# A decoder trunk's attention: where the first query tile's scores and values stand in TensorE's order

## Chip, cores and metric

One Trainium2 chip, one of its cores. The metric is the device time of one execution in microseconds (us), as the median of several runs. Beside it there is one execution taken by the hardware profiler; all rows of engines, waits and instructions come from that one. In the profile PE is TensorE (PEld its weight loads), DVE is VectorE, ACT is ScalarE, POOL is GpSimd and SP is SyncE. "L730" is line 730 of the kernel.

## The reference

Two layers over a sequence of 512 rows of width 1024, in float32. Each layer is a mixer and then a gated MLP with a short convolution, each between two RMS norms. The mixer projects its input once, and the columns feed three groups: four heads of differential attention, four of retention, and a pooling mixer. Only the attention is touched here:

```python
def block(args):
    q_blk, i = args                      # one tile of 128 queries
    s = jnp.einsum('bhmqd,bhmkd->bhmqk', q_blk, k) * scale   # m: two maps per head
    p = jax.nn.softmax(jnp.where(mask, s, -jnp.inf), axis=-1)
    a = p[:, :, 0] - lam * p[:, :, 1]
    return jnp.einsum('bhqk,bhkd->bhqd', a, v)
...
o = rms_norm(o, subln_g) * (1.0 - lam_init)
```

A head has two score maps; the second softmax is taken from the first, times a learned factor, and the difference weighs the values. The mask is causal, so query tile 0 sees only key tile 0, tile 1 two of them, and so on.

## The kernel before

All large products are done as three TensorE products of split operands (high x high, high x low, low x high), 128 x 128 by 512 columns each; these are the main products. A layer has 2256 of them: 480 for the input projection, 192 for the output projection, 1056 up and 528 down. The input projection goes through five blocks of 96: queries (products 0 to 96), keys (96 to 192), values (192 to 288), retention's queries to values (288 to 384), gates and pooling (384 to 480).

Attention and retention are small work, put between the main products. TensorE's order is fixed: every product and every turn (a transpose on TensorE) gets a dependency on the one before (`in_order`, L332). The small work comes as generators, the tasks. Each yields a place, counted in main products, and the names of what must be done ahead of it. After each group of three main products `serve` runs those that are due, the one with the earliest place first:

```python
def serve(columns=0):
    now[0] += columns / 512
    while True:
        due = [tk for tk in tasks if tk[1] <= now[0] and all(n in done for n in tk[2])]
        if not due:
            return
        with ahead(300):
            resume(min(due, key=lambda tk: tk[1]))
```

The places are read from the table `PLACE` (L45), the same for both layers, offset by 2256. So a place that has passed, or lies ahead of the time when its task is created, means "at the next group". The other engines' order is made by the scheduler of the framework from priorities and a model of times; only TensorE's is written out.

The tasks of attention, for a query tile i and a head h (in the order of tiles, then heads):

- "a", `scores` and `unit_a` (L716): two short TensorE products for one map (high and low part of the queries), in one of two PSUM banks in turn; then DVE adds the mask (L730) and takes the row maximum (L731), ACT the exponential with its sums (L733). After the second map DVE joins the two (L738 to L740).
- "b", `turns` and `unit_b` (L742): TensorE turns the joined weights, ACT copies them to SBUF (L749). It waits in order for the values two heads before.
- "c", `values` and `unit_c` (L752): TensorE multiplies the turned weights with the values. All four heads of a tile share one bank, kept for this. After head 3 the tile is normalised: four squares with sums on ACT (L766), then a row of small DVE operations (L767, and L394 to L402 in `rsqrt`), and L770 writes the normalised tile.
- "e", `outputs` and `unit_e` (L781): TensorE turns that normalised tile, and it is split into the output projection's operand.

The tasks are created after the key block, at product 192. The queries and keys of each tile are turned and split by tasks of their own ("Q", "K" in the first layer, "q", "k" in the second; `qk_done` L636, `q_split` L658, `k_split` L667); a score needs those of the tiles it sees, and at least tiles 0 and 1. Weights come over SP's queue as tiles of 512 KB, three in flight, and are split by ACT (L300) and DVE (L301) as the main products free their slots.

Of the kernel before, what the change touches and what calls it, by code (L numbers as in the profile page):

```python
# [54 lines left out]
    ],  # L55
    "b": [[234, 235, 232, 242], [275, 278, 280, 287], [326, 334, 338, 320], [381, 385, 388, 418]],
    "c": [[241, 236, 242, 243], [282, 260, 284, 296], [330, 342, 326, 350], [386, 402, 397, 427]],
    "e": [264, 317, 373, 452],
    "rows": 404,
    "r1": [395, 431, 465, 513],  # L60
# [1137 lines left out]
```

## Time and profile before

| | |
|---|---|
| median of 3 runs | 1148.23 us (1146.52 to 1148.41) |
| the profiled execution, time | 1146.27 us |
| its span, first to last instruction | 1144.5 us |
| TensorE busy | 1133.6 us, 99% of the span |
| DVE busy | 738.4 us, 65% |
| ACT busy | 547.9 us, 48% |
| DMA, mean over the span | 95 GB/s |
| mean granted TensorE clock | 0.999 |

The span runs from the first to the last instruction; the time has what lies around it too. In timeline rows the first number is the start in us from the span's start, the second the length in us; "out<-in" are the kernel's names of tiles, "x3" merges three instructions in a row, and the brackets tell how long the engine stood idle before the row and what it waited for. Matmuls are pipelined, and their ends are modelled, so the distance from start to start is the measure of what a product costs on TensorE.

### The profile page before, as it was taken

To read this page: it belongs to the slowest core of one execution; us is meant where nothing else is said; L and a number is where in the kernel's file an instruction comes from. 1 tells how busy PE (TensorE), PEld (TensorE's weight loads), DVE (VectorE), ACT (ScalarE), POOL (GpSimd) and SP (SyncE) were. 2 spreads that over 40 slices of the span, in tenths; PEclk is the share of its full clock that TensorE was granted. 3 is DMA by queue.
4 is the path that set the end of the run, shared out by engine and by line. 5 is a ranking of instruction groups with operands and counts; after the bars stand their busy time and mean duration, and the time that the engine had idled before them with its cause. 6 is when DMAs were issued, how large, how long until landed. Compare 5 with 4: busy or idle time off the path is not lost.

```text
span 1144.5 us, 14829 instructions
## 1 busy us (share of the span) xinstructions
PE 1133.6 (99%) x5474; PEld 944.9 (83%) x5474; DVE 738.4 (65%) x1667; ACT 547.9 (48%) x1051; POOL 11.9 (1%) x20
## 2 busy tenths in 40 slices
PE   9999999999999999999999999999999999999997
PEld 7788878988888888888888888789888888888886
DVE  6988796776566457423777896876856655663224
ACT  6965544564454345313367754454645434452221
POOL 1000000000000000000000000000000000000000
PEclk9999999999999999999999999999999999999999
DMA  8411131332322333324023111313333233223311
GB/s 327 146 58 56 56 116 38 111 129 97 107 92 92 99 104 97 96 93 146 1 98 123 56 57 54 111 39 117 121 99 104 81 104 103 100 76 109 96 50 58
DMA packets 31320, 109.22 MB, mean 95 GB/s; under 512 B 3728, under 2 KB 4240, under 8 KB 31248
## 3 DMA queue, kind: packets, MB, share of 16 engines
q1 hardware_dynamic: 29808, 105.11, 27.5%
q10 hardware_dynamic: 1440, 3.17, 0.8%
q8 instruction: 43, 0.70, 0.3%
q14 instruction: 29, 0.24, 0.1%
HBM read 106.16 MB, written 2.10 MB: 95 GB/s over the span
## 4 chain that ended last, share of the span: by engine, by line
PE 94%; DVE 3%; ACT 2%; issue 0%; DMA 0%; DVEq 0%; ACTq 0%
PE ps L338 74%; PE ps_m L338 12%; PE ps_o L338 2%; PE ps_b L338 2%; PE ps_b L341 2%; PE ps_s L338 1%; PE ps L341 1%; DVE ks L670 1%; ACT t L733 0%; DMA raw<-in_wout 0%; DVE sm L731 0%; DVE ps_s L730 0%; ACT ks L669 0%; ACT t L642 0%; ACT wa L300 0%
## 5 line engine op out<-in xcount | busy, mean ns | idle before, releaser
L338 PE MATMUL ps<-ht,wb 128*128 128x512 f32 (+1 forms) x1176 | 304.8, 368 | 0.0
L338 PE MATMUL ps<-ht,wa 128*128 128x512 f32 (+1 forms) x1176 | 304.7, 367 | 0.0
L338 PEld LDWEIGHTS ps<-ht,wa 128*128 128x128 f32 x1176 | 210.3, 188 | 36.5
L338 PEld LDWEIGHTS ps<-ht,wb 128*128 128x128 f32 x1176 | 210.2, 189 | 36.6
L301 DVE SCALAR_TENSOR_TENSOR wa<-raw,par,wa 128x512 fp32r<-128x512 f32 x128 | 95.7, 748 | 142.6 <-ACT wa L300 142.3
L300 ACT ACTIVATE wa<-raw,par 128x512 fp32r<-128x512 f32 x128 | 92.1, 721 | 185.0 <-PE ps L338 173.4
L338 PE MATMUL ps<-wa,c 128*128 128x512 f32 x448 | 126.2, 393 | 0.0
L290 DVE TENSOR_TENSOR wb<-raw,wa 128x1024 fp32r<-128x1024 f32 x38 | 46.5, 1225 | 81.9 <-ACT wa L289 81.9
L338 PEld LDWEIGHTS ps<-wa,c 128*128 128x128 f32 x448 | 83.6, 188 | 18.0 <-issue 1.0
L301 DVE SCALAR_TENSOR_TENSOR wb<-raw,par,wb 128x512 fp32r<-128x512 f32 x128 | 95.6, 747 | 4.0 <-ACT wb L300 3.8
L338 PE MATMUL ps<-wa,ht 128*128 128x512 f32 x352 | 97.9, 392 | 0.0
L300 ACT ACTIVATE wb<-raw,par 128x512 fp32r<-128x512 f32 x128 | 91.9, 719 | 4.3 <-PE ps L338 3.1
L338 PE MATMUL ps_m<-wa,ht 128*128 128x512 f32 x288 | 83.6, 398 | 1.8 <-ACT t L642 1.8
L338 PE MATMUL ps_m<-wb,ht 128*128 128x512 f32 x288 | 83.3, 397 | 0.0
L289 ACT CAST wa<-raw 128x1024 fp32r<-128x1024 f32 x38 | 39.9, 1051 | 86.7 <-PE ps L338 86.7
L1068 ACT ACTIVATE t<-ps,par 128x512 f32<-128x512 f32 x88 | 67.4, 773 | 24.9 <-PE ps L338 24.9
L338 PEld LDWEIGHTS ps<-wa,ht 128*128 128x128 f32 x352 | 66.2, 189 | 13.9 <-issue 0.4
L1069 DVE SCALAR_TENSOR_TENSOR t<-ps,par,t 128x511 f32<-128x511 f32 x88 | 65.2, 745 | 11.8 <-ACT t L1068 11.7
L338 PE MATMUL ps<-wb,c 128*128 128x512 f32 x224 | 71.8, 397 | 0.0
L338 PE MATMUL ps<-wb,ht 128*128 128x512 f32 x224 | 66.2, 389 | 0.0
L1070 DVE SCALAR_TENSOR_TENSOR t<-ps,par,t 128x510 f32<-128x510 f32 x88 | 65.0, 745 | 1.3
L338 PEld LDWEIGHTS ps_m<-wb,ht 128*128 128x128 f32 x288 | 52.5, 188 | 10.1
(194 smaller groups left out, 1415.3 us busy)
## 6 DMA issues: line engine op xcount, KB each, us to landing
raw<-in_wup SPq DMA_DIRECT2D x88, 512.0 KB, 3.5
raw<-in_wdown SPq DMA_DIRECT2D x44, 512.0 KB, 3.4
raw<-in_win SPq DMA_DIRECT2D x39, 512.0 KB, 3.6
raw<-in_wout SPq DMA_DIRECT2D x16, 512.0 KB, 3.4
xs<-in_x SPq DMA_DIRECT2D x4, 512.0 KB, 9.1
gain<-in_gpost ACTq DMA_DIRECT2D x4, 512.0 KB, 4.1
t<-in_xt SPq DMA_DIRECT2D x3, 512.0 KB, 5.7
out<-xs SPq DMA_DIRECT2D x4, 256.0 KB, 2.0
```

The source lines that it names most:

```text
L289: se.copy(h, r)
L290: ve.tensor_tensor(out=lo, in0=r, in1=h.bitcast(F32), op=ALU.subtract)
L300: se.activation(a, x, AF.Copy, scale=sc)
L301: low = ve.scalar_tensor_tensor(b, x, sc, a.bitcast(F32), op0=ALU.mult, op1=ALU.subtract)
L338: in_order(te.matmul(out, lhsT=lhsT, rhs=rhs, **k))
L341: in_order(te.transpose(out, in_, ident))
L670: ve.tensor_tensor(out=ks[o, :, m, sl], in0=bv[r], in1=ks[r, :, m, sl].bitcast(F32), op=ALU.subtract)
L1068: se.activation(acc, ps, AF.Identity, bias=conv[:, f, 3:4], scale=conv[:, f, 2:3])
L1069: ve.scalar_tensor_tensor(acc[:, 1:S], ps[:, 0:S - 1], conv[:, f, 1:2], acc[:, 1:S], op0=ALU.mult, op1=ALU.add)
L1070: ve.scalar_tensor_tensor(acc[:, 2:S], ps[:, 0:S - 2], conv[:, f, 0:1], acc[:, 2:S], op0=ALU.mult, op1=ALU.add)
```

## The change

Six numbers of the table move, nothing else. For query tile 0 the first score (head 0, first map) goes from place 152 to 199. Turns of heads 2 and 3 go from 232 and 242 to 242 and 246. Values of heads 1, 2 and 3 go from 236, 242 and 243 to 244, 249 and 253. Head 0's turn and value (234, 241), head 1's turn (235), all other scores and the other query tiles stay, and so does the turn of tile 0's normalised output ("e", 264). It holds for both layers.

```diff
     "a": [
-        [[152, 202], [208, 214], [221, 225], [191, 214]],
+        [[199, 202], [208, 214], [221, 225], [191, 214]],
         [[240, 240], [250, 224], [262, 241], [270, 272]],
...
-    "b": [[234, 235, 232, 242], [275, 278, 280, 287], [326, 334, 338, 320], [381, 385, 388, 418]],
-    "c": [[241, 236, 242, 243], [282, 260, 284, 296], [330, 342, 326, 350], [386, 402, 397, 427]],
+    "b": [[234, 235, 242, 246], [275, 278, 280, 287], [326, 334, 338, 320], [381, 385, 388, 418]],
+    "c": [[241, 244, 249, 253], [282, 260, 284, 296], [330, 342, 326, 350], [386, 402, 397, 427]],
     "e": [264, 317, 373, 452],
```

Lists of "a" are by tile, head and map; of "b" and "c" by tile and head; of "e" by tile.

## The prediction

> **What bounds the kernel now.** I read the page first, then the waits of PE, then the timelines of PE, DVE and ACT around the moved steps, in both layers. The page says who carries the time (busy time, granted clock in 40 slices, the shares of the chain that ended last):
>
> ```profile
> span 1144.5 us, 14829 instructions
> ...
> PE 1133.6 (99%) x5474; PEld 944.9 (83%) x5474; DVE 738.4 (65%) x1667; ACT 547.9 (48%) x1051; POOL 11.9 (1%) x20
> ...
> PEclk9999999999999999999999999999999999999999
> ...
> PE 94%; DVE 3%; ACT 2%; issue 0%; DMA 0%; DVEq 0%; ACTq 0%
> ```
>
> PE is the bound, and its order is written by hand, so a wait of PE lengthens the kernel by its own size, and what delays another engine costs nothing until PE needs the result. The waits of PE and of its weight loads show which moved steps it waits for already (total, times, longest):
>
> ```profile
> PE ps_s L338 <- DVE ks L670: 0.4, 1, 0.4
> ...
> PEld ps_o L338 <- ACT t L749: 1.1, 4, 0.4
> ...
> PEld ps_b L341 <- DVE t L770: 0.4, 2, 0.2
> ```
>
> The reader is to see the last row: twice, once per layer, the turn of the first tile's normalised output (unit_e, L341) waits for the instruction that writes it (L770). That chain has no slack today, and the change starts it later.
>
> **The change part by part: the first score.** The tasks exist only from product 192 on, and PE asks for due work every 3 products. So the first score runs at 195 today whether its place says 152 or 192, and at 201 with 199: two groups of three products later, not 47. PE in layer 0, then DVE:
>
> ```profile
> 54.27 0.84 PE L338 MATMUL ps_m<-wa,ht 128*128 128x512 f32 x3
> 55.49 0.50 PE L338 MATMUL ps_s<-ks,c 128*128 128x256 f32 x2 [0.38 <-DVE ks L670]
> ...
> 57.91 0.60 PE L341 MATMUL ps_b<-cst,t 128*128 128x128 f32 x4
> ```
>
> ```profile
> 54.75 0.69 DVE L670 TENSOR_TENSOR ks<-ps_b,ks 64x512 fp32r<-64x512 f32 x1 [0.18 <-ACT ks L669]
> ...
> 57.48 0.23 DVE L627 TENSOR_TENSOR t<-rt 128x64 f32<-128x64 f32 x1
> ```
>
> The group at 54.27 would end at 54.97 (0.70 a group, from 70.13 to 70.83 in the rows below); the score starts at 55.49 because its keys are written at 55.44. Two groups later, near 56.3, the keys are there and the wait of 0.5 us goes. What is late next is the turn of key tile 2 at 57.91: its input is finished by L627 at 57.71, so PE comes to that turn about 0.65 us earlier and waits again until about 57.8. DVE is then busy almost without pause until 70. I count the gain in layer 0 as 0.1, with 0 and 0.65 as its ends. In layer 1 the first score did not wait, but its follower does:
>
> ```profile
> 624.18 0.74 DVE L301 SCALAR_TENSOR_TENSOR wb<-raw,par,wb 128x512 fp32r<-128x512 f32 x1
> ```
>
> ```profile
> 624.34 1.28 ACT L733 ACT_TABLE_LOAD   x1 [1.02 <-DVE sm L731]
> 625.63 0.37 ACT L733 ACTIVATE t<-ps_s,sm 128x128 f32<-128x128 f32 x1
> ```
>
> ```profile
> 626.15 0.50 PE L338 MATMUL ps_s<-ks,c 128*128 128x256 f32 x2
> ```
>
> The first exponential of the layer loads a table (1.28 us) and ends at 626.00; the third score (626.15) reuses its PSUM bank, so there is no slack. A score that PE gives 1.4 us later keeps that end only if DVE takes its mask and maximum at once; if the weight split of 0.74 us gets ahead of them, the third score waits some 0.7 us. I take 0.1, ends 0 and 0.7. It cancels the 0.1 of layer 0.
>
> **The values.** Today at product 243 PE gives c0, b2, c1, b3, c2 and c3 in one go (c: values of a head, b: its turning). With the new places: 243 c0 and b2; 246 c1 and b3; 249 c2; 252 the pair of scores (tile 1, head 1), as before; 255 c3; 264 the pair of scores (head 2) and then unit_e, as before. The layer 0 rows of PE:
>
> ```profile
> 70.13 0.85 PE L338 MATMUL ps_m<-wa,ht 128*128 128x512 f32 x3
> 70.83 0.38 PE L338 MATMUL ps_o<-vv,t 128*128 128x128 f32 x2
> 71.05 0.27 PE L341 MATMUL ps_b<-cst,t 128*128 128x128 f32 x1
> 71.16 0.39 PE L338 MATMUL ps_o<-vv,t 128*128 128x128 f32 x2
> ...
> 71.80 0.75 PE L338 MATMUL ps_o<-vv,t 128*128 128x128 f32 x4
> 72.31 0.94 PE L338 MATMUL ps_m<-wb,ht 128*128 128x512 f32 x3
> 73.09 0.85 PE L338 MATMUL ps_m<-wa,ht 128*128 128x512 f32 x3
> ...
> 74.46 0.52 PE L338 MATMUL ps_s<-ks,c 128*128 128x256 f32 x3
> ...
> 74.93 0.86 PE L338 MATMUL ps_m<-wa,ht 128*128 128x512 f32 x3
> ...
> 77.68 0.52 PE L338 MATMUL ps_s<-ks,c 128*128 128x256 f32 x3
> ...
> 78.32 0.66 PE L341 MATMUL ps_b<-cst,t 128*128 128x128 f32 x4
> ```
>
> A value costs 0.22 (70.83 to 71.05), a turn 0.11 (71.05 to 71.16), a pair of scores 0.47 (74.46 to 74.93). c1 and b3 should end at 71.49, but c2 starts at 71.80: it waits 0.31 for the copies of the turns. That wait goes in both layers, since a turn and its value are now at least 3 products apart. The new course from 70.83, groups at 0.69: c0, b2 and a group 1.02; c1, b3 and a group 1.02; c2 and a group 0.91; scores and a group 1.16; then c3, after which the next group shows 0.14 later (its 0.22 less 0.08, since a group after such a product shows 0.78, as from 72.31 to 73.09). So the group behind c3 stands at 75.08 instead of 72.31. Three groups (0.78, 0.69, 0.69) and the scores (0.47) later, at 77.70, PE is ready for unit_e.
>
> unit_e's input takes its own time behind c3, four squares on ACT (L766) and a dependent row of small DVE operations (L767 to L770):
>
> ```profile
> 72.59 0.28 ACT L766 ACTIVATE t<-ps_o 128x128 f32<-128x128 f32 x1
> ```
>
> ```profile
> 73.76 0.16 DVE L767 TENSOR_TENSOR sm<-sm,sm 128x4 f32<-128x4 f32 x1 [0.31 <-ACT t L766]
> 73.96 0.17 DVE L394 TENSOR_SCALAR sm<-sm 128x4 int32<-128x4 int32 x1
> ...
> 77.58 0.68 DVE L770 TENSOR_TENSOR t<-ps_o,sm 128x512 f32<-128x512 f32 x1
> ```
>
> From 72.31 to L770's end at 78.26 that is 5.95 us, and the turn follows at 78.32. The same chain in layer 1 and for the next two query tiles, each as the group behind c3 on PE and then its L770 on DVE:
>
> ```profile
> 638.64 0.95 PE L338 MATMUL ps_m<-wb,ht 128*128 128x512 f32 x3
> ...
> 90.20 0.94 PE L338 MATMUL ps_m<-wb,ht 128*128 128x512 f32 x3
> ...
> 110.16 0.95 PE L338 MATMUL ps_s<-ks,c 128*128 128x512 f32 x3
> ```
>
> ```profile
> 643.93 0.68 DVE L770 TENSOR_TENSOR t<-ps_o,sm 128x512 f32<-128x512 f32 x1
> ...
> 94.71 0.69 DVE L770 TENSOR_TENSOR t<-ps_o,sm 128x512 f32<-128x512 f32 x1
> ...
> 115.89 0.68 DVE L770 TENSOR_TENSOR t<-ps_o,sm 128x512 f32<-128x512 f32 x1
> ```
>
> These are 5.97, 5.20 and 6.41 us. The shortest that I can build is without other DVE work in between: 0.28 to the squares, 1.17 for them, eleven small operations at 0.20, and L770's 0.68: 4.33. I take 5.95, the row of the same tile, because the same weight splits and scores lie around it; the ends are 4.33 and 6.41. From 75.08 the input is ready at 81.03, the turn starts at 81.08 instead of 78.32: 2.76 us later (1.14 to 3.22), a PE wait of about 3.4 us. Waits removed ahead of it are in this sum already, since it follows PE's own positions.
>
> Behind the waiting turn on PE stand the main products 265 on and all later work; no slack there gives it back, since PE is full to the end. ACT and DVE go on meanwhile. Nothing moved issues a DMA: SP's loads hang on the main products and their splits, in the same number and order; POOL's memsets are untouched. Tile 1's first value, at product 282, needs the bank that L770 frees and comes 18 products behind the turn, as before.
>
> The sum: 2 x 2.76 = 5.5, the first score 0. The profiled execution of 1146.27 would become 1151.8; it lies 2 us under the median, so the median of 1148.23 becomes 1153.7.
>
> **The rivals.** (a) The chain shortens: DVE finds nothing to put between, 1.14 per layer, and the first score's 0.65 is kept: +1.6, 1149.9. For it: DVE has its waiting work done while PE stands. Against it: in all four rows above it took 5.2 us or more. (b) Other side: unit_e's wait stays hidden and only the old waits go: 0.5 at the keys, 0.31 and 0.1 of restart twice, 0.2 at L770 twice: -1.7, 1146.5. It decides from the point where c3 to L770's end takes 2.6 us or less (75.08 to 77.70). No row is near it. (c) After a wait of 3.4 us the array starts slowly, as it did at the start of the kernel:
>
> ```profile
> 1.19 4.45 PE L338 MATMUL ps_o<-t 128*128 128x512 bf16 x10 [1.19 <-DVE t L527]
> ...
> 31.33 0.96 PE L338 MATMUL ps_m<-wa,ht 128*128 128x512 f32 x3 [1.76 <-ACT t L642]
> 32.13 0.85 PE L338 MATMUL ps_m<-wb,ht 128*128 128x512 f32 x3
> ```
>
> The first ten products took 0.44 each, against 0.23 later, with the granted clock shown full. After the wait of 1.76 us at 31.33 three took 0.80: no slow start. Ten slow ones would cost 2.1 us a layer: +9.8, 1158.0. The Trainium skill ("TensorE: Matmul & The Clock Gate", "What's actually happening") says that an idle window of about 3.4 us sets the array back to half its clock; by it a window lost would cost about 1.7 us a layer (an estimate from that page), and since the windows run free, a wait barely as long would rarely fill one. The slow start agrees with that rule; no wait in this trace is long enough to test it.
>
> **How the numbers follow.** A difference under 0.2% (2.3 us) can't be told from none by a measurement of this kernel. Forecast, +3.5 to +7.5: 0.78. Rival (a), ending within 0.2%: 0.08. Rival (b), 0.05, of which 0.02 beyond 0.2% faster. Rival (c) 0.07. The remaining 0.02 I give to an unforeseen gain in the DVE order. So slower 0.85, same 0.11, faster 0.04. The range runs from rival (a), 1149.9, to the long chain with the 0.7 of layer 1 (2 x 3.22 + 0.7 = 7.1, 1155.4) and a part of rival (c): 1150 to 1156.5. Where the time is slower, it is the likeliest case's own range, 1151.7 to 1155.7.
>
> **What would show it.** Right: PE's wait list gains "ps_b L341 <- DVE t L770" with 2 waits of about 3 us each; the PE rows near 71 show values one by one, and the 0.31 before c2 is gone; the wait for ks (L670) is gone, and the turn near 57.8 waits for L627. Wrong: the waits for L770 are under 1 us, or the products behind them run at 0.44 each (c), or the third score of layer 1 waits over 1 us. The forecast falls if the order of PE at 255 to 264 isn't as walked, or if L767 to L770 runs without anything between.

## The result and the profile after

The changed kernel takes 1161.35 us (median of 4 runs, 1160.22 to 1162.47), the kernel before 1148.24 beside it: ratio 1.012, 95% interval 1.0108 to 1.0132. That is 13 us slower, where 5.5 were forecast. The profiled execution took 1160.65 us, against 1146.27. From the page after: the span, the busy times, and the chain that ended last.

```profile
span 1158.9 us, 14831 instructions
...
PE 1138.0 (98%) x5474; PEld 947.9 (82%) x5474; DVE 739.3 (64%) x1667; ACT 548.3 (47%) x1051; POOL 11.9 (1%) x20
...
PE 93%; DVE 3%; DMA 1%; ACT 1%; issue 0%; SPq 0%; DVEq 0%; ACTq 0%
```

The work is the same, 5474 products and 1667 operations on DVE. But the span grew by 14.4 us while PE's busy time grew by 4.4: PE waited 10 us longer and was also busy longer for the same products. Its waits in the changed kernel (total, times, longest) say where the first part went:

```profile
PE ps_b L341 <- DVE t L770: 9.7, 2, 4.9
...
PE ps_s L338 <- ACT t L733: 0.6, 1, 0.6
PE ps_b L341 <- DVE t L627: 0.5, 1, 0.5
```

The turn of tile 0's output waits 4.9 us for L770, once in each layer. PE's timeline around it, layer 0, answers to the rows of before from 70.13 to 78.32:

```profile
72.72 0.38 PE L338 MATMUL ps_o<-vv,t 128*128 128x128 f32 x2
...
73.75 0.38 PE L338 MATMUL ps_o<-vv,t 128*128 128x128 f32 x2
...
74.78 0.39 PE L338 MATMUL ps_o<-vv,t 128*128 128x128 f32 x2
...
75.70 0.51 PE L338 MATMUL ps_s<-ks,c 128*128 128x256 f32 x3
...
76.86 0.38 PE L338 MATMUL ps_o<-vv,t 128*128 128x128 f32 x2
77.00 0.95 PE L338 MATMUL ps_m<-wb,ht 128*128 128x512 f32 x3
...
79.17 0.51 PE L338 MATMUL ps_s<-ks,c 128*128 128x256 f32 x3
...
84.66 1.12 PE L341 MATMUL ps_b<-cst,t 128*128 128x128 f32 x4 [4.86 <-DVE t L770]
85.43 1.63 PE L338 MATMUL ps_m<-wa,ht 128*128 128x512 f32 x3
86.86 1.27 PE L338 MATMUL ps_m<-wb,ht 128*128 128x512 f32 x3
87.97 0.86 PE L338 MATMUL ps_m<-wa,ht 128*128 128x512 f32 x3
```

The values come one by one as placed, the wait before c2 is gone, and c3 is followed by three groups and a pair of scores. Behind the wait three products take 1.43 us (85.43 to 86.86); behind the same turn in the kernel before they took 0.78 (78.73 to 79.51). The same profile's stages, with the columns span, busy time of PE, PEld, DVE, ACT and POOL, granted clock, DMA share and GB/s, show why: first two stretches near the start of the kernel, then one behind the wait in each layer.

```profile
29.72:33.14 3.42, 1.65 (x8) 1.28 (x8) 3.36 (x12) 3.37 (x6) 0.00 (x0) 1.00 0.41 145
33.14:36.55 3.41, 3.41 (x10) 2.67 (x9) 3.37 (x10) 3.27 (x8) 0.00 (x0) 0.50 0.43 150
...
84.70:87.00 2.30, 2.30 (x8) 2.01 (x9) 0.57 (x1) 0.59 (x1) 0.00 (x0) 0.50 0.18 73
...
657.60:659.00 1.40, 1.40 (x6) 1.30 (x7) 0.00 (x0) 0.50 (x1) 0.00 (x0) 0.56 0.43 173
```

The granted clock behind the waits is 0.50, and a product takes 0.43 us there instead of 0.23. The 40 slices of the page are too coarse to show it, and PE counts as busy all the while.

Lining up the main products of the two profiles gives the account of the 14.4 us. At the first queries' products the changed kernel is 1.8 behind, 1.5 of it from half clock after the wait of 1.8 us at 31.6. That wait is in both kernels and stands ahead of everything that moved; the slow products behind it also appear in half of the profiles below, with either order, so I don't count them to the change (the last section says when they come). The layer 0 turn then stands 6.3 behind, and 7.7 once the slow products are past. In layer 1 the turn is 12.9 behind, and 14.4 after the slow products. So the turns account for 4.5 and 5.2 (0.7 of the 5.2 is lost earlier in layer 1, at its third score), the slow products for 1.4 and 1.5.

Why the wait is 4.9 and not 3.4 is on ACT and DVE. First the changed kernel's ACT, then its DVE, and last the exponential of the same pair of scores in the kernel before:

```profile
77.25 0.48 ACT L733 ACTIVATE t<-ps_s,sm 128x256 f32<-128x256 f32 x1 [0.63 <-DVE sm L731]
...
77.72 0.47 ACT L733 ACTIVATE t<-ps_s,sm 128x256 f32<-128x256 f32 x1
...
78.16 0.27 ACT L766 ACTIVATE t<-ps_o 128x128 f32<-128x128 f32 x1
```

```profile
79.61 0.30 DVE L730 TENSOR_TENSOR ps_s<-ps_s,cst 128x128 f32<-128x128 f32 x1 [0.37 <-PE ps_s L338]
79.82 0.15 DVE L767 TENSOR_TENSOR sm<-sm,sm 128x4 f32<-128x4 f32 x1
...
81.77 0.73 DVE L301 SCALAR_TENSOR_TENSOR wb<-raw,par,wb 128x512 fp32r<-128x512 f32 x1
...
83.92 0.69 DVE L770 TENSOR_TENSOR t<-ps_o,sm 128x512 f32<-128x512 f32 x1
```

```profile
76.56 0.47 ACT L733 ACTIVATE t<-ps_s,sm 128x256 f32<-128x256 f32 x1 [1.18 <-DVE sm L731]
```

The group behind c3 starts at 77.00, but the squares start at 78.16 and not 0.28 later. On ACT they stand behind the two exponentials of the pair of scores that PE now gives ahead of c3, and those wait for their maxima on DVE. In the kernel before the same exponentials came at 76.56, 2.8 us after the squares had ended. The squares end at 79.3, and L767 then stands behind a mask (L730) that waits for the next pair of scores. From 77.00 to L770's end at 84.61 the chain takes 7.61 us, against 5.95 before.

### The profile page after: what moved, and what is told of

It reads as the page before. It is cut to its first block, busy times and chain, and to the rows that moved or that the text cites. A ratio compares the mean times of both kernels' runs of the same rounds, so it can differ in the third digit from the quotient of the medians.

```text
span 1158.9 us, 14831 instructions
## 1 busy us (share of the span) xinstructions
PE 1138.0 (98%) x5474; PEld 947.9 (82%) x5474; DVE 739.3 (64%) x1667; ACT 548.3 (47%) x1051; POOL 11.9 (1%) x20
## 4 chain that ended last, share of the span: by engine, by line
PE 93%; DVE 3%; DMA 1%; ACT 1%; issue 0%; SPq 0%; DVEq 0%; ACTq 0%
PE ps L338 72%; PE ps_m L338 13%; PE ps_b L341 2%; PE ps_s L338 2%; PE ps_b L338 2%; PE ps_o L338 2%; PE ps L341 1%; DMA raw<-in_wout 1%; DMA raw<-in_win 1%; DVE wb L301 0%; DVE space L301 0%; DVE ks L670 0%; ACT wa L300 0%; DVE ps_s L730 0%; DVE sm L731 0%
## 5 line engine op out<-in xcount | busy, mean ns | idle before, releaser
L338 PE MATMUL ps_m<-wa,ht 128*128 128x512 f32 x288 | 86.3, 409 | 1.8 <-ACT t L642 1.8
L338 PEld LDWEIGHTS ps_m<-wa,ht 128*128 128x128 f32 x288 | 53.1, 195 | 11.5 <-ACT t L642 2.2
```

The costliest lines, as they stand in the source:

```text
L338: in_order(te.matmul(out, lhsT=lhsT, rhs=rhs, **k))
```

## The experiments

All edit the same table of places, in both layers. "Before" beside a ratio is the kernel before, run on the same chip.

**all_e285.** The change, with the turn of the output at 285.

```diff
-    "e": [264, 317, 373, 452],
+    "e": [285, 317, 373, 452],
```

> The changed table with one more number moved: the turn of tile 0's normalised output goes from place 264 to 285. Theory (the loss is PE's wait for L770 at that turn, 4.9 us a layer, and the slow products behind it, with 0.8 us at layer 1's third score beside it): both waits for L770 and the products at 0.43 us behind them are gone; 0.8 stays, and the old waits (0.41 at c2 and 0.2 at L770, per layer) stay away: about 1147.8, between 1146.5 and 1149.5. Rival (the spread values themselves disturb the order on DVE and ACT, wherever the turn stands): most of the loss stays, 1155 or more.

Measured: ratio 1.0016 (1.0007 to 1.0025), some 1.8 us over before. The turn no longer waits for L770, and there is no half clock in the attention. So nearly all of the loss hangs on that one wait. What its trace still has is the wait at the third score of layer 1 (0.7) and a new wait of 0.7 in each layer, less the small waits that went. PE and DVE of this kernel:

```profile
85.56 1.13 PE L338 MATMUL ps_o<-vv,t 128*128 128x128 f32 x8 [0.72 <-ACT vv L673]
```

```profile
82.65 0.74 DVE L301 SCALAR_TENSOR_TENSOR wa<-raw,par,wa 128x512 fp32r<-128x512 f32 x1
...
84.73 0.68 DVE L770 TENSOR_TENSOR t<-ps_o,sm 128x512 f32<-128x512 f32 x1
```

With the turn out of the way, one more weight split got into the chain and L770 ends at 85.41. Tile 1's first value (place 282) waits 0.72: its bank is free only when L770 has read it. The profile names an ACT instruction (L673) that ends at 85.57, but PE starts at 85.56, and L673 writes the values of key tile 2, which tile 1 doesn't use; in the kernel before the same products ran from 83.89 while L673 ran from 84.11 to 84.80. So by the times it is L770, though no run separates the two. The time of 1149.34 lies at the range's upper edge, but over the kernel before of this chip it is +1.8 where -0.4 was expected: the chain has a second user, and I hadn't counted it.

**score_only and values_only.** One half of the change each.

```diff
 score_only:  -[[152, 202], ...   +[[199, 202], ...          ("a"; "b" and "c" as before)
 values_only: "b" and "c" as in the change                   ("a" as before)
```

> Only the first score moves (152 to 199), turns and values as in the kernel before. Theory: its only lasting cost is at layer 1's third score, which waits 0.7 to 0.9 us for the exponential behind the table load; layer 0 wins the wait for ks (0.5) and gives it to the turn of key tile 2: +0.5 to +1, about 1149. Rival (the later first score upsets DVE's order up to the normalisation): PE waits for L770 for more than 1 us, 1152 or more.

> Only the turns and values of tile 0 move, the first score stays at 152. Theory: two waits for L770 of about 5 us and slow products behind them; 0.8 less than the change as a whole, about 1160.5 (1159 to 1161.5). Rival (the two moves act together, the late first score making the chain longer): under 1157, with waits for L770 under 4 us.

Measured: score_only 1.0009 (1.0 to 1.0018), about +1; values_only 1.0123 (1.0109 to 1.0137), 1161.49. The moved turns and values make the whole loss, with two waits for L770 of 10.0 us in total and a chain of 7.6 and 7.9 us. The first score costs what it costs in layer 1, here in score_only:

```profile
628.28 0.51 PE L338 MATMUL ps_s<-ks,c 128*128 128x256 f32 x2 [0.65 <-ACT t L733]
```

values_only came out 1 us above its point and inside its range. Its profile has more products at 0.43 us (10 and 9 behind the two waits, against 4 and 5 with the whole change), and none at the start, where the changed kernel's had 7.

**before_e252 and before_e258.** The kernel before with only the turn moved, earlier. Values and scores are not spread.

```diff
-    "e": [264, 317, 373, 452],
+    "e": [252, 317, 373, 452],       (258 in the other)
```

> The kernel before with one number moved: the turn of tile 0's normalised output at place 252 instead of 264. Scores, turns and values stand as before, so nothing is spread; only the distance from the last value to the turn shrinks to three groups of products and a pair of scores, as in the changed kernel. Theory (the distance alone makes the loss): the chain stays near 6.0 us, PE comes to the turn at about 74.9 and waits 3.3 us a layer for L770, and the next ten or so products run at 0.43 us at half granted clock (2 us and more a layer): +9 to +11 over the kernel before. Rival (the spread values make it): within 2 us of the kernel before.

> The same with the turn at 258: PE comes to it at about 76.3 and waits 1.9 us a layer. Theory A (the array slows only behind waits of 3 us or more): no products at 0.43 us behind the wait, +3.4 over the kernel before. Theory B (a wait of under 2 us can be enough, as at 31.6 in the changed kernel's profile, where it was 1.8): slow products behind at least one of the two waits, +5 to +8, and runs that differ by 2 us and more.

Measured: 1.0081 (1.0067 to 1.0095), +9.3, and 1.003 (1.0019 to 1.0041), +3.4. PE of before_e252, a stage of its layer 1, then PE of before_e258:

```profile
78.72 1.11 PE L341 MATMUL ps_b<-cst,t 128*128 128x128 f32 x4 [3.23 <-DVE t L770]
79.49 1.63 PE L338 MATMUL ps_m<-wa,ht 128*128 128x512 f32 x3
```

```profile
649.80:653.00 3.20, 3.17 (x10) 2.69 (x11) 1.44 (x4) 0.59 (x1) 0.00 (x0) 0.50 0.53 166
```

```profile
79.99 0.66 PE L341 MATMUL ps_b<-cst,t 128*128 128x128 f32 x4 [1.84 <-DVE t L770]
80.40 0.94 PE L338 MATMUL ps_m<-wa,ht 128*128 128x512 f32 x3
```

Both waits came out as worked out from the chain of 5.95: 3.2 for 3.3, 1.8 for 1.9. The distance on PE alone makes a loss, without any value spread. And the pair prices the clock. Behind 1.8 us the products run at full speed, and the time is the waits' (3.7 less the 0.3 that PE waited before). Behind 3.2 us the clock is 0.50: in the profiled execution, 11.1 over that of before, 6.1 are longer waits and 4.2 slow products (1.6 and 2.6 by layer). Theory A is right for these two waits; but the profile of before_e258 has seven slow products behind the wait of 1.8 us near 31, which the turn has nothing to do with.

**all_s11_late and all_scores_late.** The change, with the pair of scores of tile 1, head 1 behind c3; in the second also the pair of head 2 behind the turn.

```diff
-        [[240, 240], [250, 224], [262, 241], [270, 272]],
+        [[240, 240], [257, 224], [262, 241], [270, 272]],     all_s11_late
+        [[240, 240], [257, 257], [266, 266], [270, 272]],     all_scores_late
```

> The changed table with the first map's score of tile 1, head 1 moved from place 250 to 257, so that this pair of scores runs behind the last value of tile 0 and no longer ahead of it. Theory (the normalisation takes 7.6 us and not 6.0 because its squares stand on ACT behind the exponentials of that pair): the squares start 0.3 us behind the value and not 1.0, the chain is 6.0 to 6.4, and with the value 0.47 earlier PE waits 2.9 to 3.4 us a layer and not 4.9: about 1157.5. Rival (the chain is long through DVE's own order): it stays at 7.3 us or more, the wait at 4.4 or more, 1160 or more.

> The changed table with both pairs of scores that stand around the chain moved behind it: tile 1's head 1 at 257 (behind the last value of tile 0) and head 2 at 266 (behind the turn). Theory (what PE gives DVE and ACT while the chain runs makes its length): the squares start 0.1 us behind the value, DVE has only weight splits and the one pair to put between, the chain is 5.0 to 6.0 us, PE waits 2.2 to 3.2 us a layer, and the time is 8 to 11 over the kernel before. Rival (the chain stays at 7.4 us, as with head 1 alone moved): wait 4.5, +13 or more.

Measured: 1.0106 (1.0091 to 1.0122) and 1.0097 (1.0083 to 1.0111). PE, ACT and DVE of all_s11_late, then PE and DVE of all_scores_late:

```profile
75.69 0.94 PE L338 MATMUL ps_m<-wb,ht 128*128 128x512 f32 x3
...
79.07 0.84 PE L338 MATMUL ps_s<-ks,c 128*128 128x256 f32 x3 [0.59 <-ACT t L733]
...
83.18 1.12 PE L341 MATMUL ps_b<-cst,t 128*128 128x128 f32 x4 [3.16 <-DVE t L770]
```

```profile
75.97 0.28 ACT L766 ACTIVATE t<-ps_o 128x128 f32<-128x128 f32 x1 [0.19 <-PE ps_o L338]
```

```profile
77.14 0.17 DVE L767 TENSOR_TENSOR sm<-sm,sm 128x4 f32<-128x4 f32 x1
...
82.44 0.69 DVE L770 TENSOR_TENSOR t<-ps_o,sm 128x512 f32<-128x512 f32 x1
```

```profile
76.38 0.94 PE L338 MATMUL ps_m<-wb,ht 128*128 128x512 f32 x3
...
82.94 1.11 PE L341 MATMUL ps_b<-cst,t 128*128 128x128 f32 x4 [3.77 <-DVE t L770]
```

```profile
82.20 0.69 DVE L770 TENSOR_TENSOR t<-ps_o,sm 128x512 f32<-128x512 f32 x1
```

Half of the theory held. With the pair behind c3 the squares start 0.28 after the group (75.69 to 75.97), so it was the exponentials that held them. But the chain hardly shrinks: L767 to L770 now takes 5.30 us, since three masks and four maxima of the two pairs, one join and two splits stand in it; 7.44 in all, as the rival had it. My range of 6.0 to 6.4 failed, and the time too. The wait of 3.16 lies in the theory's range by luck: PE has already waited 0.59 for a score bank ahead of the turn. With both pairs out of the way the chain is 6.5 (76.38 to 82.89), again with two splits and one pair in it; above the range of 5.0 to 6.0. PE needs 2.8 from the group behind c3 to the turn, as the theory had it, so the wait is 3.8 and not 2.2 to 3.2 because of the chain alone, and the time is 11.1 over before, where 8 to 11 were expected. The direction is right, the size is not.

**all_e273.** The change, with the turn at 273.

> The changed table with the turn at 273 instead of 264, three groups of products later. If the chain from value to L770 keeps its 7.6 us, the wait shrinks from 5.0 to 2.8 us a layer. With the half clock behind it as before: about 4.4 less than the changed kernel, +10 over the kernel before; without it: +6. If the chain stretches because more work of DVE gets in between, as it did with the turn at 285 (8.5 us), the wait is nearer 3.5 and the time nearer +12.

Measured: 1.0084 (1.0069 to 1.01), +9.6. The chain stretched to 8.1 us, the waits are 3.26 in both layers, and the products behind them run at half clock. Nine more products of distance, about 2.1 us of PE, took only 1.6 off each wait, since the chain grew with them: the case of the nearer 3.5 and +12, with a little less time.

**tuned and tuned_e279.** From the kernel before: values of heads 2 and 3 at 246, tile 1's first pair at 243, the turn at 270 or 279.

```diff
-        [[240, 240], ...                 +        [[243, 243], ...
-    "c": [[241, 236, 242, 243], ...      +    "c": [[241, 236, 246, 246], ...
-    "e": [264, ...                       +    "e": [270, ...        (279 in the other)
```

> A version that takes the small waits of the kernel before and leaves its first score: values of heads 2 and 3 at 246 (from 242 and 243), the turn of the output at 270 (from 264), tile 1's first pair of scores at 243 (from 240). Theory: the waits at c2 (0.3), for the score bank (0.3) and for L770 (0.2) go in both layers, and the last value comes only 0.6 later while the turn comes 1.4 later: 1.0 to 1.8 less than the kernel before. Rival (DVE puts a weight split of 0.75 into the chain, or PE waits elsewhere): within 0.5 of the kernel before, or slower.

> The version before this (values of heads 2 and 3 at 246, tile 1's first pair of scores at 243) with the turn of the output at 279 instead of 270. There PE had won 0.9 us a layer ahead of the turn and lost it to a wait of 1.2 us for L770, since the squares stood 1.4 us behind the exponentials of the moved pair. With the turn three groups later the wait is gone and the 0.9 stays: 1.3 to 1.8 less than the kernel before. Rival (the chain only stretches with the turn, or another wait follows, as with the turn at 285): within 0.5 of the kernel before.

Measured: 1.0006 (0.9997 to 1.0015) and 1.0001 (0.9992 to 1.001). PE of tuned, then PE of tuned_e279:

```profile
72.37 0.94 PE L338 MATMUL ps_m<-wa,ht 128*128 128x512 f32 x3
...
80.31 0.66 PE L341 MATMUL ps_b<-cst,t 128*128 128x128 f32 x4 [1.23 <-DVE t L770]
```

```profile
84.57 0.38 PE L338 MATMUL ps_s<-ks,c 128*128 128x256 f32 x1 [0.81 <-ACT t L733]
```

The small waits went and PE was 0.7 to 1.2 us ahead before the turn. In tuned the moved pair's exponentials again stood ahead of the squares: the chain is 7.9 and the gain went back at L770. In tuned_e279 it went back at the next score, which waits for its bank behind an exponential. Neither beats the kernel before.

## Why the prediction was wrong, point by point

Its sign, its place and its mechanism were right: slower, through PE's wait for L770 at the turn, in both layers, with PE's order exactly as walked. The time lies outside the range, by three terms.

**The chain: mis-sized, 5.95 taken, 7.61 measured (7.60 in layer 1).** The step that failed is "because the same weight splits and scores lie around it". The range's upper end was 6.41, the longest of the four rows, and those rows belong to another order on ACT and DVE. In all four the squares started within 0.35 us of the group behind c3. all_s11_late shows the exponentials as the cause of the late squares, but not as the whole: the row from L767 to L770 took between 3.8 us and 5.3 for this tile, with what PE and the splits gave DVE meanwhile. No run separates the parts of that. The difference is 1.66 a layer, 3.3 in the sum. The position of c3 was right: 75.08 forecast, 77.00 less the 1.8 of the start measured.

**The half clock: put among the rivals with 0.07, and it was the case.** The step that failed is the chance. The prediction worked out a wait of 3.4 us and then let one row, the wait of 1.76 without slow products, speak for it. That row was luck: in six of the twelve profiles the same wait is followed by seven or eight slow products. In the changed kernel they begin only in the third group behind it (33.09 after 31.60), so the one group that the prediction read couldn't rule them out. Nor was the clock "shown full" at the kernel's first ten products a measurement: the clock record of that trace begins at 6.13, behind them. The price of 2.1 us a layer was high: 1.4 and 1.5 here. before_e258 and before_e252 show that for this turn the step lies between waits of 1.8 and 3.2 us.

**Layer 1's third score: 0.1 taken, 0.8 measured.** The end given was 0.7, for a split getting ahead of the mask. That happened: DVE takes a split at 631.30 and the mask (L730) only at 632.34. ACT of the changed kernel, then PE:

```profile
633.05 1.28 ACT L733 ACT_TABLE_LOAD   x1 [1.81 <-DVE sm L731]
634.34 0.37 ACT L733 ACTIVATE t<-ps_s,sm 128x128 f32<-128x128 f32 x1
```

```profile
633.61 0.60 PE L341 MATMUL ps_b<-cst,t 128*128 128x128 f32 x4
634.85 0.50 PE L338 MATMUL ps_s<-ks,c 128*128 128x256 f32 x2 [0.65 <-ACT t L733]
```

Together: 5.5, with 3.3 for the chain, 2.9 for the slow products and 0.7 for the third score, makes 12.4 of the 13.1 measured.

**Right:** the first score comes two groups later, not 47 products. The layer 0 wait for ks went, and the turn of key tile 2 took it over; PE of the changed kernel:

```profile
58.21 0.40 PE L338 MATMUL ps_s<-ks,c 128*128 128x256 f32 x2
...
59.75 0.63 PE L341 MATMUL ps_b<-cst,t 128*128 128x128 f32 x4 [0.45 <-DVE t L627]
```

The wait at c2 (0.31 in both layers) went too and gave nothing, as the sum had it, since the turn behind it is what PE waits for. Rival (b) was rightly judged far off.

## What to carry to other kernels

Before moving work on the bound engine, find the chain that starts at it and the place where the bound engine needs its end: here the row with "PEld ... <- L770, 2 times" already said that there was no slack. Don't take such a chain's length from the old order when the order on the other engines is the scheduler's: list what the move puts ahead of each link (an exponential, a mask that waits) and make the range from that, not from the spread of the old rows. And if the worked-out wait of TensorE is 1.8 us or more, give the products at half clock behind it a real chance; behind each of the twelve waits of 3.1 us or more here they came.

## What the runs showed of the hardware

The half clock comes behind waits shorter than I had thought. In all six profiles with a wait of 3.1 us or more at the turn, products behind it took 0.43 us, in both layers, with the granted clock down to 0.50. How many varied from 2 to 10. Behind 1.2 and 1.8 us at the turn none did. But behind the wait of 1.8 us near 31 seven or eight products took 0.43 in 6 of 12 profiles (the granted clock was 0.50 from 33.14 to 36.55 in the changed kernel), and none in the other six.

The clock records of the traces show what decides. In one profile the granted clock changes only at times that lie a whole number of 3.413 us apart: 33.14, 36.55, 84.34, 87.75, 657.78 and 661.19 in the changed kernel. The changed kernel's two stages near the start, shown above, are such periods; these are the kernel before's:

```profile
30.02:33.43 3.41, 2.10 (x9) 1.76 (x10) 3.35 (x12) 3.38 (x6) 0.00 (x0) 1.00 0.25 99
33.43:36.84 3.41, 3.41 (x19) 2.83 (x18) 3.37 (x13) 3.35 (x9) 0.00 (x0) 1.00 0.60 175
```

The wait is as long in both, but PE idles 1.77 us of one period in the changed kernel (3.42 less 1.65) and 1.31 in the kernel before, where part of the wait lies ahead of the period. In the twelve traces each full-clock period in which PE idled 2.1 us or more was followed by one at half clock, none with 1.7 us or less was, and of nine with 1.77 to 1.84 us six were. A second period at half clock followed where PE still idled 0.86 us or more in the first, which is why the number of slow products varies. So between 1.8 us and some 4.2 (twice 2.1, an estimate from these figures) it depends on where a wait falls. The Trainium skill ("TensorE: Matmul & The Clock Gate", "What's actually happening") lets the clock fall after at least one idle window of about 3.4 us, with windows that run free. The free windows and their length agree with these traces; that the whole window must be idle does not, since 2.1 of 3.41 us were enough. What decides among the nine stays open.
